# Three of eight experts computed in plain float32, with the raw weights as the stationary operand of the matmuls

## The chip, the core and the metric

The kernel runs on one core of a Trainium2 chip. The metric is the device time of one execution in microseconds (us). Before the change the median of three runs is 1679.45 us (1677.75 to 1680.64). Inside the core, TensorE (PE) multiplies matrices, and its weight loads are a row of their own in the profile (PEld); VectorE (DVE) and ScalarE (ACT) do elementwise work; GpSimd (POOL) does a little; SyncE (SP) issues the transfers (DMA) from HBM, the chip's main memory.

## The reference

The reference is a trunk of two layers over 256 tokens of width 1024, all in float32. Layer 0 has a mixer, a cross-attention to memory tokens and a dense SwiGLU; layer 1 has another mixer, another cross-attention, and a mixture of eight SwiGLU experts of width 3584. This last part, on the normalised tokens `t`, takes the second half of the time:

```
logits = t @ w_router                       # 256 x 8
top_v, top_i = top_k(logits, 2)             # two experts per token
combine = one_hot(top_i) * softmax(top_v)   # weight of each expert for each token
for e in range(8):
    out += combine[:, e] * ((silu(t @ wg[e]) * (t @ wu[e])) @ wd[e])
```

The weights of an expert are 1024x3584 (gate), 1024x3584 (up) and 3584x1024 (down). All eight have to be read, about 352 MB in float32.

## The kernel before, in words

**Number format.** [...] To hold the precision the kernel splits each operand into a high and a low part: `wh` is the rounded weight, which ACT writes (line 120, two calls of 1024 columns for a piece), and `wl` is the remainder, which DVE writes (line 122, one call of 2048 columns). A piece is 1 MB of weights, 128x2048, in one of 13 `raw` buffers; three pairs of `wh`/`wl` exist (pool `wsplit`, `bufs=3`). A product is then three matmuls: high by high (line 137), low activations by high weights (line 140), high activations by low weights (line 143), in `mm3`.

**Experts.** A token goes to two experts only. The kernel sorts the experts by how many tokens chose them (`places`, line 859) and puts them at positions 0 to 7 of the loop `for e in range(NE)`. Positions in `SMALL` take the three experts with the fewest tokens, with 64 slots for tokens (`SCAP`); the others have 128 slots (`CAP`). If an expert had more, code behind the loop would do the rest; it is not entered here.

**Chunks.** Each expert runs in seven chunks of 512 of its 3584 columns. A chunk reads six pieces: gate (two halves), up (two halves), down (two halves). `gate_up` multiplies the gathered tokens by gate and up; `gated` applies SiLU and the product; `to_hT` transposes the result; `down` multiplies the previous chunk's result by the down weights into `yacc`. So PE's order in a chunk is gate, up, the down of the chunk before, transposes.

**Large experts.** The tokens are the stationary operand (128 slots wide), and 512 columns of the weights move past them. A chunk is 24 matmuls for gate, 24 for up and 24 for down, each of 512 columns.

**Small experts, before.** The high and the low part of 64 slots lie side by side in one stationary tile of 128 columns, so that a product needs two matmuls (`mm2`, line 985: by `wh`, by `wl`): 16 for gate, 16 for up, 16 for down. ACT copies both results to SBUF (`sgs`, line 1019); eight float32 matmuls by the constant `twice` (line 1036) transpose them and add the two halves; then SiLU (line 1038), the product (line 1039) and a split (`hs`, lines 128 and 129).

**Around the experts.** `gather_pair` (line 934), in the last chunk of every second expert, picks the tokens of the next two experts by matmuls with one-hot matrices; `slot_rstd` (line 963) fetches the norm factor of each slot; `slots_T` (line 972) and `scatter` (line 1066) add an expert's result back to the residual `x`.

**Order.** The order of instructions on each engine is written when the program is built and is the same in each execution; an engine takes its instructions strictly in that order and waits when an operand is not there. SP issues the loads of the pieces in turn, and waits before each for the release of the `raw` buffer that it fills.

Of the kernel before, what the change touches and what calls it, by code (L numbers as in the profile page):

```python
# [11 lines left out]
F32 = mybir.dt.float32  # L12
# [22 lines left out]
SCAP = 64  # L35
SMALL = (2, 4, 6)
LAM_INIT = 0.8 - 0.6 * math.exp(-0.3)
# [17 lines left out]
def trunk_kernel(ctx: ExitStack, tc: tile.TileContext, io, out, stop=None):  # L55
# [151 lines left out]
    def route_consts():  # L207
# [20 lines left out]
        nc.gpsimd.iota(iota, pattern=[[1, P]], base=0, channel_multiplier=0, allow_small_or_imprecise_dtypes=True)  # L228
        iota2 = cp.tile([P, 2, SCAP], F32, tag="iota2", name="iota2")
        nc.gpsimd.iota(iota2, pattern=[[0, 2], [1, SCAP]], base=0, channel_multiplier=0,  # L230
                       allow_small_or_imprecise_dtypes=True)
        place = cp.tile([P, 4, 2], F32, tag="place", name="place")
        nc.gpsimd.iota(place, pattern=[[1, 4], [4, 2]], base=0, channel_multiplier=0,
                       allow_small_or_imprecise_dtypes=True)
        return wr, gc, tri, ustr, ones, iota, iota2.rearrange("p a b -> p (a b)"), place.rearrange("p a b -> p (a b)")

    pA = ctx.enter_context(tc.tile_pool(name="acts", bufs=1))
    ps2 = ctx.enter_context(tc.tile_pool(name="xs", bufs=2))
    with ExitStack() as pre:
# [526 lines left out]
        with behind("resid", "Pool"):  # L766
            wr, gc, tri, ustr, ones, iota, iota2, place = route_consts()
        mem_v_half(1, 0)
# [3 lines left out]
    with ExitStack() as moe:  # L772
# [140 lines left out]
        def slots(dst, t, e):  # L913

            at = byp[:, t, e:e + 1] if ids[1] is not None else pos[:, t, e:e + 1]
            chain["DVE"] = nc.vector.tensor_scalar(dst, iota2 if e in SMALL else iota, at, None, op0=OP.is_equal)

        def gained(kk, e, n, src):

            dh, dl = (xg_all[i][:, 0:n, kk, :] for i in range(2))  # L920
            g1 = gc[:, kk:kk + 1]
            chain["ACT"] = nc.scalar.activation(dh, src, AF.Copy, scale=g1)
            for i in range(n):
                if e + i in SMALL:
                    dst = hi = dh[:, i, SCAP:P]
                    rows = src[:, i, SCAP:P]
                else:
                    dst, hi, rows = dl[:, i, :], dh[:, i, :], src[:, i, :]
                chain["DVE"] = nc.vector.scalar_tensor_tensor(dst, rows, g1, hi.bitcast(F32), op0=OP.mult, op1=OP.subtract)

# [3 lines left out]
        def gather_pair(e):  # L934

            n = min(2, NE - e)
            se = m2.tile([P, 2, 2, P], F32R, tag="sg", name="sp", bufs=1)
            for t in range(2):
                for i in range(2):
                    slots(se[:, t, i, :], t, min(e + i, NE - 1))  # L940
            for q in range(4):
                if q < 2:
                    ps = mbank([P, 2, 2, P], "xg")
                else:
                    ps = accp.tile([P, 2, 2, P], F32, tag="acc", name="xg")
                for k in range(2):
                    kk = 2 * q + k
                    sl = slice(kk * P, (kk + 1) * P)
                    for t in range(2):
                        nc.tensor.matmul(ps[:, k, :, :], xh[t][:, sl], se[:, t, :, :], start=t == 0, stop=False)  # L950
                        nc.tensor.matmul(ps[:, k, :, :], xl[:, t, sl], se[:, t, :, :], start=False, stop=t == 1)
                    gained(kk, e, n, ps[:, k, 0:n, :])

# [3 lines left out]
        def one_hot(e):  # L957
            se = m2.tile([P, 2, P], F32, tag="sg", name="so", bufs=1)
            for t in range(2):
                slots(se[:, t, :], t, e)  # L960
            return se
# [10 lines left out]
        def slots_T(e):  # L972
            se = one_hot(e)
            tp = mbank([P, 2, P], "setp")
# [3 lines left out]
            nc.scalar.activation(st, tp, AF.Copy)  # L978
            return st

        def gate_piece(w, e, c, half):
            return load_w(w[ids[e], half * 512:(half + 1) * 512, c * 512:(c + 1) * 512]
                          .rearrange("(k p) n -> p k n", p=P), 4, 512)

        def mm2(jobs, first, last):

            for which in range(2):
                for i, (ps, a, *b) in enumerate(jobs):
                    f = first and which == 0 and all(j[0] is not ps for j in jobs[:i])
                    e = last and which == 1 and all(j[0] is not ps for j in jobs[i + 1:])  # L990
                    mm = nc.tensor.matmul(ps, a, b[which], start=f, stop=e)  # L991
            return mm

        def gate_up(e, c, xg, ready=(), between=None):
            xgh, xgl = xg
            res = []
            ready = list(ready)
            for w in (wg, wu):
# [4 lines left out]
                for half in range(2):  # L1003
                    wh, wl = ready.pop(0) if ready else gate_piece(w, e, c, half)
                    if e in SMALL:
                        mm = mm2([(ps, xgh[:, half * 4 + k, :], wh[:, k, :], wl[:, k, :]) for k in range(4)],
                                 half == 0, half == 1)
                    else:
                        mm = mm3([(ps, xgh[:, half * 4 + k, :], xgl[:, half * 4 + k, :], wh[:, k, :], wl[:, k, :])
                                  for k in range(4)], False, half == 0, half == 1)  # L1010
                res.append(ps)
# [14 lines left out]
        def down_w(e, c, parts=1):  # L1026
            return [load_w(wd[ids[e], c * 512 + half * 256:c * 512 + half * 256 + 256, :]
                           .rearrange("(k p) n -> p k n", p=P), 2, D, parts) for half in range(2)]

        def to_hT(e, sg, pool=pA, tag="gain"):  # L1030
            if e in SMALL:

                tp = mbank([P, 2, 4, SCAP], "htp")
                for i in range(2):
                    for k in range(4):
                        nc.tensor.matmul(tp[:, i, k, :], sg[:, i, k * P:(k + 1) * P], twice, start=True, stop=True)
                h = m2.tile([P, 4, SCAP], F32, tag="hsm", name="hsm", bufs=1)
                nc.scalar.activation(h, tp[:, 0, :, :], AF.Silu)
                nc.vector.tensor_tensor(h, h, tp[:, 1, :, :], op=OP.mult)
                hs = pool.tile([P, 4, P], F32R, tag=tag, name="hs")  # L1040
                chain["hh"], chain["hl"] = split_to(hs[:, :, 0:SCAP], hs[:, :, SCAP:P], h)
                return hs, None
            tp = mbank([P, 4, P], "htp")
# [7 lines left out]
        def down(c, hT, yacc, w2, ns=(0, 1)):  # L1051
            hh, hl = hT
            if hl is None:
                return mm2([(yacc[n], hh[:, half * 2 + k, :], w2[half][0][:, k, n * 512:(n + 1) * 512],
                             w2[half][1][:, k, n * 512:(n + 1) * 512])
                            for half in range(2) for n in ns for k in range(2)], c == 0, c == nch - 1)
            return mm3([(yacc[n], hh[:, half * 2 + k, :], hl[:, half * 2 + k, :],
# [3 lines left out]
        def split_y(yacc, n, pool=mA, tag="y"):  # L1061
            y = pool.tile([P, 2, 512], F32R, tag=tag, name="y")
            split_to(y[:, 0, :], y[:, 1, :], yacc[n])
            return y
# [47 lines left out]

        twice = mA.tile([P, SCAP], F32, tag="twice", name="twice")
        for i in range(2):
            nc.gpsimd.tensor_copy(twice[i * SCAP:(i + 1) * SCAP, :], ident[i * SCAP:(i + 1) * SCAP, i * SCAP:(i + 1) * SCAP])
        prev = y = st = nrs = pyacc = gf = None
        for e in range(NE):
            for c in range(nch):
# [3 lines left out]
                def between():  # L1122
# [4 lines left out]
                    elif c == 4:  # L1127
                        st = slots_T(e)
                    elif c == nch - 1 and e + 1 < NE:
                        nrs = slot_rstd(e + 1)  # L1130
# [28 lines left out]
                if c == 0:  # L1159
                    yacc = [mmp.tile([P, 512], F32, tag="mm", name=f"y{n}") for n in range(2)]  # L1160
                hT = to_hT(e, sg) if e + 1 < NE or c + 1 < nch else to_hT(e, sg, mA, "y")
# [130 lines left out]
```

## Time and profile before

| what | value |
|---|---|
| median of three runs | 1679.45 us |
| the profiled execution's own time | 1674.53 us |
| its span (first to last instruction) | 1672.8 us |
| PE busy, matmuls | 1581.7 us (95%) |
| PE busy, weight loads | 1300.4 us (78%) |
| DVE busy | 1263.6 us (76%) |
| ACT busy | 1077.1 us (64%) |
| TensorE clock granted, mean | 0.996 |
| read from HBM | 461.90 MB |

The span starts and ends with instructions; the execution's own time is 1.7 us longer. The profiled execution is 4.9 us below the median of the runs shown. The eight experts take about the last 1030 us. [...]

### The profile page before, as it was taken

The page shows a single profiled execution, that of the slowest core. Times are in us where ns is not written, and L with a number is a line of the kernel's source. Part 1 is how long each engine was busy: PE and PEld are TensorE (multiplying, and loading weights), DVE is VectorE, ACT ScalarE, POOL GpSimd, SP SyncE. Part 2 cuts the span into 40 slices and gives each one's busy share as a digit, 9 for nine tenths or more (in the row PEclk, how much of TensorE's full clock was granted, in tenths as well). Part 3 has the DMA queues.
Part 4 walks back from the last instruction along what each step waited for, and adds up shares of the span by engine and source line. Part 5 has one row for each costly group of instructions (what it writes and reads, how often), then busy time and mean ns, then how long its engine had stood idle before and what let it go on. Part 6 is the DMA issues. An engine that isn't in the chain of part 4 may idle for free. (4 is left out here: it accounts for less than half of the span.)

```text
span 1672.8 us, 22375 instructions
## 1 busy us (share of the span) xinstructions
PE 1581.7 (95%) x8448; PEld 1300.4 (78%) x8448; DVE 1263.6 (76%) x1214; ACT 1077.1 (64%) x1396; POOL 46.9 (3%) x68
## 2 busy tenths in 40 slices
PE   8999999999999999999999889998889998889996
PEld 7799889999988888888887567776557776557774
DVE  5785664454586658989888789788779878878876
ACT  5555553443564447877777777777777667778765
POOL 1010010000000102000000000000000000000000
PEclk9999999999999999999999999999999999999998
DMA  6556465555545597999999999999999999999960
GB/s 234 164 175 215 144 225 194 180 195 177 190 126 183 195 340 268 352 373 333 365 360 359 344 337 348 334 343 333 362 342 339 342 342 334 356 346 332 340 258 27
DMA packets 224560, 464.49 MB, mean 278 GB/s; under 512 B 9074, under 2 KB 64390, under 8 KB 224316
## 3 DMA queue, kind: packets, MB, share of 16 engines
q1 hardware_dynamic: 223564, 459.80, 78.1%
q0 software_dynamic: 880, 3.19, 0.6%
q8 instruction: 68, 1.11, 0.3%
q14 instruction: 48, 0.39, 0.1%
HBM read 461.90 MB, written 2.11 MB: 277 GB/s over the span
## 5 line engine op out<-in xcount | busy, mean ns | idle before, releaser
L122 DVE TENSOR_TENSOR wl<-raw,wh 128x2048 fp32r<-128x2048 f32 (+1 forms) x527 | 985.5, 1894 | 267.1 <-ACT wh L120 266.4
L120 ACT ACTIVATE wh<-raw 128x1024 fp32r<-128x1024 f32 x866 | 852.6, 1047 | 269.0 <-PE pws L140 94.9
L137 PE MATMUL gu<-wh,ch 128*128 128x512 f32 x560 | 222.0, 397 | 0.0
L140 PE MATMUL gu<-wh,cl 128*128 128x512 f32 x560 | 219.4, 392 | 0.1
L143 PE MATMUL gu<-wl,ch 128*128 128x512 f32 x560 | 155.8, 400 | 11.9 <-DVE wl L122 11.7
L143 PEld LDWEIGHTS gu<-wl,ch 128*128 128x128 f32 x560 | 101.7, 188 | 49.7 <-DVE wl L122 30.3
L140 PE MATMUL pws<-nl,wh 128*128 128x256 f32 x560 | 137.6, 283 | 0.0
L137 PE MATMUL pws<-nh,wh 128*128 128x256 f32 x560 | 137.6, 283 | 0.0
L991 PE MATMUL gu<-wl,ch 128*128 128x512 f32 x336 | 98.8, 416 | 40.1 <-DVE wl L122 40.1
L140 PEld LDWEIGHTS gu<-wh,cl 128*128 128x128 f32 x560 | 105.2, 188 | 22.2 <-DVE cl L1097 0.5
L137 PEld LDWEIGHTS gu<-wh,ch 128*128 128x128 f32 x560 | 105.2, 188 | 21.8 <-ACT hs L128 0.8
L137 PE MATMUL y<-wh,hs 128*128 128x512 f32 x280 | 112.9, 403 | 0.3 <-ACT wh L120 0.3
L991 PEld LDWEIGHTS gu<-wl,ch 128*128 128x128 f32 x336 | 57.3, 188 | 69.0 <-DVE wl L122 60.5
L140 PE MATMUL y<-wh,hs 128*128 128x512 f32 x280 | 110.4, 394 | 0.0
L137 PEld LDWEIGHTS pws<-nh,wh 128*128 128x128 f32 x560 | 106.2, 190 | 1.3 <-ACT wh L120 0.9
L140 PEld LDWEIGHTS pws<-nl,wh 128*128 128x128 f32 x560 | 106.1, 190 | 0.4
L991 PE MATMUL gu<-wh,ch 128*128 128x512 f32 x336 | 99.9, 403 | 1.5 <-ACT wh L120 1.3
L137 PE MATMUL acc<-wh,ch 128*128 128x512 f32 x216 | 84.7, 392 | 0.0
L140 PE MATMUL acc<-wh,cl 128*128 128x512 f32 x216 | 84.4, 391 | 0.0
L991 PEld LDWEIGHTS gu<-wh,ch 128*128 128x128 f32 x336 | 61.6, 188 | 22.7 <-ACT wh L120 10.2
L143 PE MATMUL pws<-nh,wl 128*128 128x256 f32 x560 | 78.8, 283 | 0.0
L143 PE MATMUL y<-wl,hs 128*128 128x512 f32 x280 | 74.6, 396 | 0.0
(363 smaller groups left out, 2197.4 us busy)
## 6 DMA issues: line engine op xcount, KB each, us to landing
raw<-in_moe_w_gate_dram SPq DMA_DIRECT2D x112, 1024.0 KB, 7.0
raw<-in_moe_w_up_dram SPq DMA_DIRECT2D x112, 1024.0 KB, 7.0
raw<-in_moe_w_down_dram SPq DMA_DIRECT2D x110, 1024.0 KB, 7.1
raw<-in_mem_w_kv_dram SPq DMA_DIRECT2D x16, 1024.0 KB, 5.5
raw<-in_odd_w_in_dram SPq DMA_DIRECT2D x12, 1024.0 KB, 5.2
raw<-in_ffn_w_gate_dram SPq DMA_DIRECT2D x11, 1024.0 KB, 5.2
raw<-in_ffn_w_up_dram SPq DMA_DIRECT2D x11, 1024.0 KB, 5.3
raw<-in_ffn_w_down_dram SPq DMA_DIRECT2D x11, 1024.0 KB, 4.7
```

The source lines that it names most:

```text
L120: chain["wh"] = nc.scalar.activation(hf[:, sl], rf[:, sl], AF.Copy)
L122: chain["wl"] = nc.vector.tensor_sub(lf[:, sl], rf[:, sl], hf[:, sl].bitcast(F32))
L137: mm = nc.tensor.matmul(ps, ah, bh, start=f, stop=False, skip_group_check=bank)
L140: nc.tensor.matmul(ps, *((ah, bl) if w_left else (al, bh)), start=False, stop=False, skip_group_check=bank)
L143: mm = nc.tensor.matmul(ps, *((al, bh) if w_left else (ah, bl)), start=False, stop=e, skip_group_check=bank)
L991: mm = nc.tensor.matmul(ps, a, b[which], start=f, stop=e)
```

## The change

The three small experts leave the split format. Their weights are no longer split: the `raw` piece itself is the stationary operand, in tiles of 128x128, and the 64 gathered tokens move past it, in plain float32. The gate, up and down results come out transposed (weights' columns on the partitions), so that the transposing matmuls, `sgs` and the split `hs` go. The norm factor of each slot is multiplied into the gathered tokens (`xsm`) rather than into the results. The accumulator `yacc` of a small expert is transposed back at its end (four transposes for each half, `split_y`). A chunk has 32 plain float32 matmuls for gate, 32 for up and 32 for down. The small positions move from 2, 4, 6 to 2, 4, 7, so that the order of experts is large, large, small, large, small, large, large, small. The last down weights are no longer loaded in two parts. The eight constants `place` are set one by one on POOL.

```diff
-SMALL = (2, 4, 6)
+SMALL = (2, 4, 7)
...
-        def gained(kk, e, n, src):
...
+        def gained(kk, e, n, src, rsrow):
+
             g1 = gc[:, kk:kk + 1]
-            chain["ACT"] = nc.scalar.activation(dh, src, AF.Copy, scale=g1)
             for i in range(n):
                 if e + i in SMALL:
...
+                    nc.vector.scalar_tensor_tensor(xsm[:, kk, :], src[:, i, 0:SCAP], g1, rsrow, op0=OP.mult, op1=OP.mult)
+                    continue
...
+            rsrow = None
+            for i in range(n):
+                if e + i in SMALL:
+                    sr = m2.tile([P, 2, SCAP], F32, tag="sr", name="sr", bufs=1)
+                    rp = mbank([P, SCAP], "rp")
+                    for t in range(2):
+                        nc.vector.tensor_scalar(sr[:, t, :], se[:, t, i, 0:SCAP].bitcast(F32), comb[:, t, NE:NE + 1], None, op0=OP.mult)
+                        nc.tensor.matmul(rp, ones, sr[:, t, :], start=t == 0, stop=t == 1)
...
+        def small_up(e, c, between):
+
+            ps = accp.tile([P, 2, 4, SCAP], F32, tag="acc", name="gu")
+            for i, w in enumerate((wg, wu)):
...
+                for half in range(2):
+                    r = load_raw(gate_src(w, e, c, half), 4, 512)
+                    for f in range(4):
+                        for k in range(4):
+                            chain["PE"] = nc.tensor.matmul(ps[:, i, f, :], r[:, k, f * P:(f + 1) * P], xsm[:, half * 4 + k, :],
+                                                           start=i == half == f == k == 0, stop=half == 1 and k == 3,
+                                                           skip_group_check=True)
+            return ps
...
             if e in SMALL:
-                sg = m2.tile([P, 2, 512], F32, tag="sgs", name="sgs", bufs=1)
-                for i in range(2):
-                    nc.scalar.activation(sg[:, i, :], res[i], AF.Copy, scale=rs)
-                return sg
+                h = m2.tile([P, 4, SCAP], F32, tag="hsm", name="hsm")
+                nc.scalar.activation(h, res[:, 0, :, :], AF.Silu)
+                nc.vector.tensor_tensor(h, h, res[:, 1, :, :], op=OP.mult)
+                return h
...
+                for half in range(2):
+                    for d in range(KT):
+                        for k in range(2):
+                            mm = nc.tensor.matmul(yacc[:, d, :], w2[half][:, k, d * P:(d + 1) * P], hh[:, half * 2 + k, :],
...
+                    yT[0] = m2.tile([P, KT, SCAP], F32, tag="yT", name="yT", bufs=1)
+                    nc.scalar.activation(yT[0], yacc, AF.Copy)
...
+                for k in range(4):
+                    nc.tensor.transpose(tp[:, k, :], yT[0][:, n * 4 + k, :], ident)
...
-        with behind("hh", "hl"):
-            w2 = down_w(pe, pc, 2)
+        w2 = down_w(pe, pc)
```

PE's order in the small expert at position 2, before: about one chunk in the middle of it. `gu` are the gate and up results, `y` the accumulator of down, `wh` and `wl` the split weights, `ch` the gathered tokens.

```order
L991 MATMUL gu<-wl,ch 128x512 x4
L991 MATMUL gu<-wh,ch 128x512 x3
L1036 MATMUL htp<-twice,sgs 128x64 x4
L991 MATMUL gu<-wl,ch 128x512 x4
L991 MATMUL gu<-wh,ch 128x512 x4
L991 MATMUL y_8179<-wh,hs 128x512
L991 MATMUL gu<-wl,ch 128x512 x4
L991 MATMUL y_8179<-wh,hs 128x512
L991 MATMUL y_8180<-wh,hs 128x512 x2
L1036 MATMUL htp<-twice,sgs 128x64 x4
```

The same place after the change; `raw` is the loaded piece, `xsm` and `hsm` the moving activations of 64 slots, `setp` belongs to `slots_T`.

```order
L1064 MATMUL y<-hsm,raw 128x64 x32
L1007 MATMUL gu<-xsm,raw 128x64 x64
L1064 MATMUL y<-hsm,raw 128x64 x32
L1007 MATMUL gu<-xsm,raw 128x64 x64
L1064 MATMUL y<-hsm,raw 128x64 x32
L1007 MATMUL gu<-xsm,raw 128x64 x32
L982 MATMUL setp<-ident,so 64x128 x2
L1007 MATMUL gu<-xsm,raw 128x64 x32
```

Fewer and wide matmuls, mixed with each other, have become 64 and 32 narrow ones in turn, with nothing of ACT's or DVE's splits in front of them.

ACT's order at the same position before: `wh` are the split weights, `hs` the split input of down.

```order
L120 ACTIVATE wh<-raw 128x1024 x4
L1019 ACTIVATE sgs<-gu,rs 128x512
L120 ACTIVATE wh<-raw 128x1024 x4
L1019 ACTIVATE sgs<-gu,rs 128x512
L120 ACTIVATE wh<-raw 128x1024 x2
L1038 ACTIVATE hsm<-htp 128x256
L120 ACTIVATE wh<-raw 128x1024 x2
L128 ACTIVATE hs<-hsm 128x4x64
```

And after, the whole small expert at position 2, up to the first splits for the large expert behind it; `ch` are the gathered tokens of that one.

```order
L1034 ACTIVATE hsm<-gu 128x256
L128 ACTIVATE y<-y_7277 128x512
L128 ACTIVATE y<-y_7278 128x512
L1034 ACTIVATE hsm<-gu 128x256 x3
L984 ACTIVATE st<-setp 64x256
L1034 ACTIVATE hsm<-gu 128x256 x2
L923 ACTIVATE ch<-xg,gc 128x128 x3
L1034 ACTIVATE hsm<-gu 128x256
L923 ACTIVATE ch<-xg,gc 128x128 x5
L120 ACTIVATE wh<-raw 128x1024 x6
```

ACT has one call of `hsm` for each of the seven chunks, and the splits of the next large expert (six calls, three pieces) stand behind all of them.

## Rows read from the trace of the kernel before

**Rows 1.** The page: busy time by engine, and the granted clock in 40 slices.
```profile
PE 1581.7 (95%) x8448; PEld 1300.4 (78%) x8448; DVE 1263.6 (76%) x1214; ACT 1077.1 (64%) x1396; POOL 46.9 (3%) x68
PEclk9999999999999999999999999999999999999998
```

**Rows 2.** Busy time by window: start:end, length, engines' busy, clock, DMA share, GB/s.
```profile
816.63:833.85 17.22, 17.22 (x80) 14.12 (x79) 15.27 (x11) 13.39 (x17) 0.00 (x0) 1.00 1.00 363
1046.24:1064.55 18.31, 17.36 (x76) 13.53 (x75) 14.74 (x9) 12.66 (x15) 0.00 (x0) 1.00 0.97 345
1174.26:1192.56 18.30, 15.04 (x65) 10.28 (x64) 14.41 (x9) 13.43 (x16) 0.00 (x0) 1.00 1.03 386
```

**Rows 3.** Who waited for whom, 645 to 1655 us: total, times, longest.
```profile
ACT sgs L1019 <- PE gu L991: 58.1, 36, 1.7
PE gu L991 <- DVE wl L122: 40.1, 56, 0.9
```

**Rows 4.** Timeline of ACT: start, length, line, operation, and idle before it.
```profile
867.74 0.67 ACT L1022 ACTIVATE sg<-gu,rs 128x512 f32<-128x512 f32 x1
...
1010.79 0.69 ACT L1022 ACTIVATE sg<-gu,rs 128x512 f32<-128x512 f32 x1 [0.48 <-PE gu L143]
1026.76 0.69 ACT L1022 ACTIVATE sg<-gu,rs 128x512 f32<-128x512 f32 x1 [1.72 <-PE gu L143]
...
1120.15 0.69 ACT L1022 ACTIVATE sg<-gu,rs 128x512 f32<-128x512 f32 x1 [2.07 <-PE rsp L967]
1138.46 0.69 ACT L1019 ACTIVATE sgs<-gu,rs 128x512 f32<-128x512 f32 x1 [1.72 <-PE gu L991]
...
1268.42 0.69 ACT L1022 ACTIVATE sg<-gu,rs 128x512 f32<-128x512 f32 x1 [0.45 <-PE gu L143]
...
1396.10 0.69 ACT L1019 ACTIVATE sgs<-gu,rs 128x512 f32<-128x512 f32 x1 [1.72 <-PE gu L991]
```

**Rows 5.** Timeline of PEld: runs of float32 weight loads, count at the end.
```profile
631.43 0.97 PEld L811 LDWEIGHTS rlp<-wr,rht 128*128 128x128 f32 x8
...
635.33 2.76 PEld L838 LDWEIGHTS xg<-se,h 128*128 128x128 f32 x24
...
890.38 1.09 PEld L1036 LDWEIGHTS htp<-twice,sgs 128*128 128x128 f32 x8
...
917.30 0.97 PEld L1036 LDWEIGHTS htp<-twice,sgs 128*128 128x128 f32 x8 [0.58 <-ACT sgs L1019]
```

**Rows 6.** Line 1036, both halves of a matmul: durations in ns (shortest/middle/longest).
```profile
L1036 PEld LDWEIGHTS htp<-twice,sgs x336: 186/192/192, 890.4 to 1518.4; 128*128 128x128 f32 x168
L1036 PE MATMUL htp<-twice,sgs x336: 217/275/323, 890.6 to 1518.4; 128*128 128x64 f32 x168
```

**Rows 7.** Timeline of PE: a large chunk's first down matmul, and the transposes behind its last.
```profile
820.87 0.40 PE L137 MATMUL y<-wh,hs 128*128 128x512 f32 x1
...
826.45 0.60 PE L1045 MATMUL htp<-ident,sg 128*128 128x128 f32 x4
```

**Rows 8.** Groups by line, whole span: the two gather matmuls of `gather_pair`.
```profile
L950 PE MATMUL xg<-sp,xh 128*128 128x256 f32 x64 | 15.6, 282 | 0.0
L951 PE MATMUL xg<-sp,xl 128*128 128x256 f32 x64 | 15.6, 281 | 0.0
```

**Rows 9.** The chain that ended last: the last matmuls of down.
```profile
1655.46 1.18 PE y L143 x5
```

**Rows 10.** Busy time by window: where the granted clock fell, and float32 loads.
```profile
550.00:552.00 2.00, 0.08 (x1) 0.12 (x1) 1.42 (x2) 0.00 (x0) 0.29 (x1) 1.00 0.58 179
553.00:554.00 1.00, 1.00 (x4) 0.81 (x3) 0.00 (x0) 0.00 (x0) 0.00 (x0) 0.50 0.80 248
...
631.00:633.00 2.00, 1.96 (x18) 1.96 (x19) 0.00 (x0) 1.57 (x5) 1.27 (x1) 1.00 0.00 0
```

**Rows 11.** Timeline of PE while the clock was at half.
```profile
554.20 0.63 PE L140 MATMUL pts<-wh,ml 128*128 128x512 f32 x1
554.63 0.63 PE L137 MATMUL pts<-wh,mh 128*128 128x512 f32 x1
```

More of the change, by code (lines that the diff above doesn't have):

```diff
@@ L228, in route_consts @@
         nc.gpsimd.iota(iota, pattern=[[1, P]], base=0, channel_multiplier=0, allow_small_or_imprecise_dtypes=True)
[L229 to L235, printed above, removed]
+        place = cp.tile([P, NE], F32, tag="place", name="place")
+        for i, r in enumerate((0, 4, 1, 5, 2, 6, 7, 3)):
+            nc.gpsimd.memset(place[:, i:i + 1], float(r))
+        return wr, gc, tri, ustr, ones, iota, place
     pA = ctx.enter_context(tc.tile_pool(name="acts", bufs=1))
@@ L951, in gather_pair @@
                         nc.tensor.matmul(ps[:, k, :, :], xl[:, t, sl], se[:, t, :, :], start=False, stop=t == 1)
[L952 removed]
+                    gained(kk, e, n, ps[:, k, 0:n, :], rsrow)
         wg, wu, wd = io["moe_w_gate"][0], io["moe_w_up"][0], io["moe_w_down"][0]
@@ L977, in slots_T, with gate_src, down_src @@
             st = m2.tile([P, 2, P], F32R, tag="st", name="st", bufs=1)
-            nc.scalar.activation(st, tp, AF.Copy)
-            return st
+            nc.scalar.activation(st[0:m], tp, AF.Copy)
+            return st[0:m]
+        def gate_src(w, e, c, half):
+            return w[ids[e], half * 512:(half + 1) * 512, c * 512:(c + 1) * 512].rearrange("(k p) n -> p k n", p=P)
         def gate_piece(w, e, c, half):
[L982 to L992, printed above, removed]
+            return load_w(gate_src(w, e, c, half), 4, 512)
+        def down_src(e, c, half):
+            return wd[ids[e], c * 512 + half * 256:c * 512 + half * 256 + 256, :].rearrange("(k p) n -> p k n", p=P)
+        def small_up(e, c, between):
+            ps = accp.tile([P, 2, 4, SCAP], F32, tag="acc", name="gu")
+            for i, w in enumerate((wg, wu)):
+                if i and between is not None:
+                    with behind("PE"):
+                        between()
+                for half in range(2):
[6 more added lines that the diff above has]
+            return ps
         def gate_up(e, c, xg, ready=(), between=None):
+            if e in SMALL:
+                return small_up(e, c, between)
             xgh, xgl = xg
@@ L1004, in gate_up @@
                     wh, wl = ready.pop(0) if ready else gate_piece(w, e, c, half)
[L1005 to L1010, printed above, removed]
+                    mm = mm3([(ps, xgh[:, half * 4 + k, :], xgl[:, half * 4 + k, :], wh[:, k, :], wl[:, k, :])
+                              for k in range(4)], False, half == 0, half == 1)
                 res.append(ps)
@@ L1026, in down_w @@
         def down_w(e, c, parts=1):
-            return [load_w(wd[ids[e], c * 512 + half * 256:c * 512 + half * 256 + 256, :]
-                           .rearrange("(k p) n -> p k n", p=P), 2, D, parts) for half in range(2)]
+            if e in SMALL:
+                return [load_raw(down_src(e, c, half), 2, D) for half in range(2)]
+            return [load_w(down_src(e, c, half), 2, D, parts) for half in range(2)]
         def to_hT(e, sg, pool=pA, tag="gain"):
             if e in SMALL:
[L1033 to L1042, printed above, removed]
+                return sg, None
             tp = mbank([P, 4, P], "htp")
@@ L1053, in down @@
             if hl is None:
-                return mm2([(yacc[n], hh[:, half * 2 + k, :], w2[half][0][:, k, n * 512:(n + 1) * 512],
-                             w2[half][1][:, k, n * 512:(n + 1) * 512])
-                            for half in range(2) for n in ns for k in range(2)], c == 0, c == nch - 1)
+                for half in range(2):
+                    for d in range(KT):
+                        for k in range(2):
+                            mm = nc.tensor.matmul(yacc[:, d, :], w2[half][:, k, d * P:(d + 1) * P], hh[:, half * 2 + k, :],
+                                                  start=c == half == d == k == 0, stop=c == nch - 1 and half == k == 1,
+                                                  skip_group_check=True)
+                return mm
             return mm3([(yacc[n], hh[:, half * 2 + k, :], hl[:, half * 2 + k, :],
@@ L1111, in final_gain @@
             return gf
-        twice = mA.tile([P, SCAP], F32, tag="twice", name="twice")
-        for i in range(2):
-            nc.gpsimd.tensor_copy(twice[i * SCAP:(i + 1) * SCAP, :], ident[i * SCAP:(i + 1) * SCAP, i * SCAP:(i + 1) * SCAP])
+        xsm = mA.tile([P, KT, SCAP], F32, tag="xsm", name="xsm")
+        yT = [None]
         prev = y = st = nrs = pyacc = gf = None
@@ L1128, in between @@
                         st = slots_T(e)
-                    elif c == nch - 1 and e + 1 < NE:
+                    elif c == nch - 1 and e + 1 < NE and e + 1 not in SMALL:
                         nrs = slot_rstd(e + 1)
@@ L1159, in trunk_kernel @@
                 if c == 0:
-                    yacc = [mmp.tile([P, 512], F32, tag="mm", name=f"y{n}") for n in range(2)]
+                    if e in SMALL:
+                        yacc = mmp.tile([P, KT, SCAP], F32, tag="mm", name="y")
+                    else:
+                        yacc = [mmp.tile([P, 512], F32, tag="mm", name=f"y{n}") for n in range(2)]
                 hT = to_hT(e, sg) if e + 1 < NE or c + 1 < nch else to_hT(e, sg, mA, "y")
```

26 lines of the change are left out of this document (16 added, 10 removed).

## The prediction

> **What bounds the kernel now.** I read the page first, then the windows, the waits, and the timelines of single engines. The page shows PE as the fullest engine at a clock that is full nearly everywhere [rows 1]. But a busy share is an average over three kinds of chunk, so the windows come next [rows 2]. A large chunk at position 1 takes 17.22 us and PE is busy in all of it: TensorE is the limit there. A small chunk takes 18.30 us with PE busy 15.04, its weight loads 10.28, DVE 14.41, ACT 13.43: no engine is full. A later large chunk takes 18.31 us and is not full either. The waits say why the small chunk is no shorter [rows 3]: ACT's `sgs` waits for PE (58.1 us, 36 times, 1.7 at the longest) and PE's matmuls by `wl` wait for DVE (40.1 us). ACT takes its instructions in order, so the splits behind `sgs` stand still too, and the loop ACT, DVE, PE, ACT sets the pace. Transfers are close behind: 345 to 386 GB/s in the windows of [rows 2], and 6.29 MB (six pieces of 1,048,576 bytes) at 386 GB/s are 16.3 us.
>
> So the splits are what a small chunk waits for. The question is what PE's own work becomes when they are gone.
>
> **What a plain float32 matmul costs.** The kernel already runs this very form: line 1036, stationary 128x128 and 64 moving columns, in float32. Its 168 matmuls (8 in each of 21 chunks) leave 336 records of each half, a load 0.19 us long [rows 6]: a float32 matmul is loaded and streamed twice. The step between two loads comes from the runs [rows 5]. The 24 of line 838, with 128 moving columns, take 2.76 us; less one load of 0.19 that is (2.76 - 0.19) / 23 = 0.1117 us. The 8 of line 1036 give (0.97 - 0.19) / 7 = 0.1114 with 64 columns, the 8 of line 811 the same 0.1114 with 8 columns. The step doesn't depend on the moving columns: the loads set it. One run of line 1036 is slower, (1.09 - 0.19) / 7 = 0.1286. I take 0.1117, from the longest run, and keep 0.1286 for the upper end.
>
> A small chunk then has 96 matmuls, 192 loads: 192 x 0.1117 = 21.45 us of PE, against 18.30 for all that a small chunk takes now. Before, it had 48 matmuls of 512 columns; 24 such matmuls take 826.45 - 820.87 = 5.58 us [rows 7], so 48 take 11.2, and the eight of line 1036 some 1.8. The change takes work from ACT and DVE, which were part of the loop, and puts about 8 us more on PE. PE is then the bound of the small experts, alone: gate, up and down of one small chunk are 7.15 us each, and SiLU and product (0.7 us and less on the idle ACT and DVE) lie beside the 7.15 us of the down matmuls.
>
> [...] The equal steps at 8, 64 and 128 columns in [rows 5] speak against counting columns here. [...]
>
> **The sum, stretch by stretch.** 21 small chunks are 4032 loads, 450 us. I follow PE between the gates' ends, which the SiLU or `sgs` calls of ACT mark [rows 4]. Below, 5.6 is a large expert's gate, up or down, 0.5 four transposes (0.60 less overlap, [rows 7]), 1.9 the eight matmuls of a scatter at 0.2325, 1.1 some ten small float32 records, 4 a gather. The gather's rows sum to 31.2 us over four gathers, 7.8 each [rows 8]; rows of neighbours overlap, so I take half.
>
> First small expert, from 867.74 to 1010.79, now 143.05 us. PE has to do: up 5.6, down 5.6, transposes 0.5, seven small chunks without the last down 150.2 - 7.15 = 143.0, the large expert's last down 5.6, scatter 1.9, small things 1.1, gather 4, the next gate 5.6. Sum 172.9, so +29.9. The next chunk, 1010.79 to 1026.76, is 15.97 now and becomes 5.6 + 7.15 + 0.5 + 0.5 + 5.6 = 19.35: +3.4.
>
> Rest of that large expert: unchanged. The order that I compared has PE's, ACT's and DVE's instructions of its later chunks exactly as before, ACT again with no piece split ahead, which is what separates 18.31 from 17.22 us in [rows 2]. Its last chunk into the small gate, 1120.15 to 1138.46, 18.31 us, becomes 5.6 + 5.6 + 0.5 + 7.15 = 18.85: +0.5.
>
> Second small expert, 1138.46 to 1268.42, 129.96 us: 150.2 less its first gate and last down, 135.9, then 5.6 + 1.9 + 1.1 + 4 + 5.6, together 154.1: +24.1, and +3.4 again in the chunk behind it.
>
> The rest, from 1396.10 to the end, 276.7 us, holds a small and a large expert whose places are exchanged. The large one first: as position 5 now, 1396.10 - 1268.42 = 127.7, and 4 for the gather that now falls into it. Then the small one: 143.0 + 5.6 + 1.9 + 0.3, and 1.2 for the broadcast of the final gain. The end: from the last down matmul, 1655.46 + 1.18 = 1656.6 [rows 9], to 1672.8 are 16.2, plus a copy of 512 columns, 0.7 as `sgs` in [rows 4], and 0.5 for transposes. Sum 301.1: +24.4. Placing a small expert last gains nothing: its last down is longer (7.15 for 5.6) and must be transposed.
>
> Total 29.9 + 3.4 + 0.5 + 24.1 + 3.4 + 24.4 = 85.7 us. Against the profiled execution's own time, 1674.5, that is 1760.2; the median of the runs shown is 4.9 above that execution, so I expect **1765 us**.
>
> The rest at nothing. POOL's eight `memset` calls are on an engine that is busy for 3% of the span [rows 1], ahead of the routing. The extra matmuls and copies for `rsrow` in the first `gather_pair` stand in a large chunk, one or two us at the most if PE waits for them. `xsm` has one buffer: DVE can't write the next small expert's tokens until the last gate and up of this one are through, and ACT's and DVE's gather work is queued behind it; it lies beside a 7.15 us down, and costs 2 us in each of two places if that cover is too short. SP's loads now wait for PE to release `raw` instead of DVE: six pieces in 21.45 us are 293 GB/s, under every rate in [rows 2], so transfers get slack.
>
> **Rivals.**
>
> *Loads hidden (faster).* If in long unbroken runs the next load slides fully under the running matmul, PE takes 192 x 64 columns at 0.2325 / 512, or 5.6 us, and the small chunk falls to the transfers, 16.3 to 17.3 us at 386 to 363 GB/s [rows 2]. Then 21 x (18.3 - 16.8) = 31 us are won: 1648. It decides from a step under 0.095 us (18.3 / 192). Against it stand the runs of 24 and 8, which are unbroken too. Chance 0.06.
>
> *The clock falls.* [...] Chance 0.08.
>
> *Slower steps.* 0.1286 for all loads [rows 5] is 4032 x 0.0169 = 68 us more, 1833; half of it, 1799. Chance 0.10.
>
> *Quick large chunks.* PE arrives from a small expert late, with ACT's splits waiting, as at position 1. If that lasts, 21 large chunks take 17.22 instead of 18.31: -23, 1742. Against it: the same order of instructions. Chance 0.14.
>
> **How the numbers follow.** The forecast holds 0.60, with 1750 to 1780 as its own range; the remaining 0.02 is for no change. The range takes in quick large chunks with some margin and the half-way case of slower steps: 1728 to 1815. The clock, the hidden loads and the worst steps, about 0.2, stay outside. A change of under 0.2%, 3.4 us, can't be told from none. Faster: 0.06. Same: 0.02. Slower: 0.92.
>
> **What would show it.** In the profile after: loads `gu<-xsm,raw` and `y<-hsm,raw` with a step near 0.112 us; PEld full in the small experts; about 150 us for seven small chunks; DVE and ACT nearly idle there; GB/s under 300; large chunks behind them still at 18.3 us; a granted clock of 1.00. A step of 0.06, or a clock of 0.5, would make the prediction wrong.

## The result and the profile after

The changed kernel takes 1814.74 us (median of four runs, 1803.97 to 1817.39); the kernel before, on the same chip, takes 1678.97 (1677.75 to 1680.64). The ratio is 1.080, 95% interval 1.075 to 1.084: 136 us slower. The forecast was 1765 with a range of 1728 to 1815: the result lies 0.3 us under its upper end, and two of the four executions lie above it. The profiled execution took 1817.39 us, its span 1815.7.

First the page after, against [rows 1]:

```profile
PE 1768.7 (97%) x11160; PEld 1575.9 (87%) x11160; DVE 979.7 (54%) x1065; ACT 802.3 (44%) x1080; POOL 46.1 (3%) x72
PEclk9899999999999999999999899999999999999965
GB/s 241 126 193 189 161 216 192 188 179 196 140 186 170 329 279 359 343 363 365 313 280 293 232 317 334 343 278 292 291 264 315 339 351 329 346 279 280 253 72 25
```

DVE and ACT have each lost some 280 us of work, as the change meant. PE and PEld have gained 187 and 276. And the row of the clock, all nines but its last slice in [rows 1], has an 8 in slice 2, another in slice 23, and ends in 6 and 5. The GB/s fall below 300 wherever a small expert runs.

The windows give the size of a chunk, in the columns of [rows 2]: a small chunk, a later large chunk, then the last chunk of the last (small) expert.

```profile
986.38:1007.82 21.44, 21.44 (x194) 21.44 (x194) 0.42 (x1) 0.38 (x1) 0.00 (x0) 1.00 0.88 297
1094.82:1113.14 18.32, 17.91 (x78) 13.82 (x77) 15.43 (x9) 12.66 (x15) 0.00 (x0) 1.00 0.88 318
1749.00:1760.00 11.00, 11.00 (x53) 11.00 (x54) 0.00 (x0) 0.00 (x0) 0.00 (x0) 0.50 0.00 0
1760.00:1780.00 20.00, 20.00 (x96) 20.00 (x95) 0.42 (x1) 0.38 (x1) 0.00 (x0) 0.50 0.00 1
```

The small chunk is 21.44 us, PE and PEld full, DVE and ACT nearly idle, clock 1.00: the forecast's 21.45 to within a hundredth. The last two rows show the same work, PE as full, at clock 0.50, with nothing to wait for. PE's timeline around them (start, duration, what):

```profile
1716.99 14.46 PE L1007 MATMUL gu<-xsm,raw 128*128 128x64 f32 x128
1731.29 7.31 PE L1064 MATMUL y<-hsm,raw 128*128 128x64 f32 x64
1738.53 1.98 PE L1130 MATMUL gfp<-gfrow,ones 1*128 1x512 f32 x4
1740.43 27.12 PE L1007 MATMUL gu<-xsm,raw 128*128 128x64 f32 x128
1767.35 27.52 PE L1064 MATMUL y<-hsm,raw 128*128 128x64 f32 x128
```

The same 128 records of gate and up take 14.46 us before `gfp` and 27.12 behind it; `gfp` are the matmuls that spread the final gain from one partition to 128. The two downs behind them take 27.52. The clock never came back before the end.

A smaller fall of the same kind stands at the gather in the first small expert:

```profile
1018.00:1021.00 3.00, 3.00 (x29) 3.00 (x29) 0.00 (x0) 0.00 (x0) 0.00 (x0) 1.00 0.85 275
1021.00:1024.00 3.00, 2.27 (x21) 2.21 (x21) 1.27 (x7) 0.00 (x0) 0.00 (x0) 1.00 0.85 279
1024.00:1027.00 3.00, 3.00 (x18) 3.00 (x16) 0.00 (x0) 0.00 (x0) 0.00 (x0) 0.53 0.83 313
1027.00:1033.00 6.00, 6.00 (x30) 6.00 (x30) 0.46 (x2) 0.37 (x1) 0.00 (x0) 0.50 0.20 52
1033.00:1036.00 3.00, 3.00 (x23) 3.00 (x22) 1.10 (x5) 0.63 (x2) 0.00 (x0) 0.77 0.67 259
```

Behind four matmuls of one moving column PE pauses 0.73 us (3.00 - 2.27) for the one-hot tiles of the gather, which DVE writes; then the clock is at half for 10 us, and comes back behind nine gather matmuls of 256 columns (1031.1 to 1033.2). The second small expert has the same for 6.8 us, from 1321.1. In the last expert, between its last matmuls of 512 columns and `gfp`, the same thin matmuls (but for two transposes) held 1.00 for 96.7 us:

```profile
1641.84:1738.53 96.69, 96.69 (x868) 96.62 (x866) 3.25 (x7) 2.30 (x6) 0.00 (x0) 1.00 0.77 261
```

### The profile page after: what moved, and what is told of

It reads as the page before. It is cut to its first block, busy times and chain, and to the rows that moved or that the text cites. A ratio compares the mean times of both kernels' runs of the same rounds, so it can differ in the third digit from the quotient of the medians.

```text
span 1815.7 us, 27052 instructions
## 1 busy us (share of the span) xinstructions
PE 1768.7 (97%) x11160; PEld 1575.9 (87%) x11160; DVE 979.7 (54%) x1065; ACT 802.3 (44%) x1080; POOL 46.1 (3%) x72
## 5 line engine op out<-in xcount | busy, mean ns | idle before, releaser
L122 DVE TENSOR_TENSOR wl<-raw,wh 128x2048 fp32r<-128x2048 f32 (+1 forms) x399 | 700.9, 1780 | 216.8 <-ACT wh L120 215.7
L120 ACT ACTIVATE wh<-raw 128x1024 fp32r<-128x1024 f32 x610 | 603.5, 1051 | 269.2 <-PE pws L140 99.1
L1007 PEld LDWEIGHTS gu<-xsm,raw 128*128 128x128 f32 x2688 | 322.3, 201 | 1.8 <-ACT gf L1131 0.8
L1007 PE MATMUL gu<-xsm,raw 128*128 128x64 f32 x2688 | 323.4, 284 | 0.0
L137 PE MATMUL gu<-wh,ch 128*128 128x512 f32 x560 | 222.2, 397 | 1.4 <-ACT wh L120 1.4
L143 PE MATMUL gu<-wl,ch 128*128 128x512 f32 x560 | 156.0, 400 | 12.2 <-DVE wl L122 11.8
L1064 PE MATMUL y<-hsm,raw 128*128 128x64 f32 x1344 | 166.4, 289 | 0.0
L1064 PEld LDWEIGHTS y<-hsm,raw 128*128 128x128 f32 x1344 | 165.4, 205 | 0.4
L143 PEld LDWEIGHTS gu<-wl,ch 128*128 128x128 f32 x560 | 101.5, 188 | 47.1 <-DVE wl L122 28.2
L137 PEld LDWEIGHTS gu<-wh,ch 128*128 128x128 f32 x560 | 105.1, 188 | 24.7 <-ACT wh L120 2.3
```

Source lines behind the costliest of these rows:

```text
L120: chain["wh"] = nc.scalar.activation(hf[:, sl], rf[:, sl], AF.Copy)
L122: chain["wl"] = nc.vector.tensor_sub(lf[:, sl], rf[:, sl], hf[:, sl].bitcast(F32))
L137: mm = nc.tensor.matmul(ps, ah, bh, start=f, stop=False, skip_group_check=bank)
L143: mm = nc.tensor.matmul(ps, *((al, bh) if w_left else (ah, bl)), start=False, stop=e, skip_group_check=bank)
L1007: chain["PE"] = nc.tensor.matmul(ps[:, i, f, :], r[:, k, f * P:(f + 1) * P], xsm[:, half * 4 + k, :], start=i == half == f == k == 0, stop ...
L1064: mm = nc.tensor.matmul(yacc[:, d, :], w2[half][:, k, d * P:(d + 1) * P], hh[:, half * 2 + k, :], start=c == half == d == k == 0, stop=c = ...
```

## The experiments

Two theories. **Clock:** the float32 step is as forecast, and what came on top is TensorE's clock: thin float32 (64 moving columns) holds a full clock but doesn't bring back a lost one, so that a small disturbance can cost many microseconds. **Not the clock:** the excess is in the placement, the gathers or the transfers, and the clock only shows it.

**1. Take the disturbance away.** The final gain is spread by a DMA, without `gfp`:

```diff
-                nc.tensor.matmul(ps, ones[0:1, :], row[:, n * 512:(n + 1) * 512], start=True, stop=True)
+            nc.sync.dma_start(gf, bcast(io["norm_final"], 0, [[1, D]]))
```

> The final gain is spread over the partitions by a DMA and no longer by PE's four one-row matmuls (gfp, 1738.53 to 1740.43 in the profile after, right ahead of the fall of the clock at 1741). Theory A: these few rows, in the middle of float32 matmuls of 64 columns, cost the full clock, and 64-column float32 holds a full clock but doesn't bring it back. Then the last 256 float32 records run at 0.112 instead of 0.21 us: 54.6 us become 28.6, and the end some 3 us shorter: 1786 us. Rival B: a long run of 64-column float32 loses the clock by itself after a while: the fall stays, 1810 to 1817.

Measured: 1792.24 us, ratio 1.064 (1.058 to 1.070). In its trace the last gate and up take 14.46 us again, and so do the last downs:

```profile
1752.25 14.46 PE L1007 MATMUL gu<-xsm,raw 128*128 128x64 f32 x128
1766.55 14.46 PE L1064 MATMUL y<-hsm,raw 128*128 128x64 f32 x128
```

That is 22.5 us less, and the falls at the gathers are still there (20.5 and 17.1 us long in this execution).

**2. Undo the placement.** `SMALL` and `place` as before, a large expert last:

```diff
-SMALL = (2, 4, 7)
+SMALL = (2, 4, 6)
```

> The changed kernel with the small experts back at positions 2, 4, 6, so that a large one is last. Theory A: the one-row matmuls fall among matmuls of 512 columns and cost no clock; three small experts cost about 88 us as forecast, and each of them some 3 to 5 us of half clock at its gather: 1775 to 1785. Rival B (the clock is lost by long runs alone): a fall in or behind position 6 that lasts until its end, 1795 or more. If the place of the small expert itself cost the time (its longer end, nothing hidden behind it), the clock would be as before and the time still under 1790: then the profile's clock tells.

Measured: 1800.39 us, ratio 1.071 (1.068 to 1.075): too high by 15 to 25. `gfp` now stands among matmuls of 512 columns and the clock stays up there. But it was at half for 17.1 us at each of two gathers:

```profile
1311.00:1314.00 3.00, 2.27 (x21) 2.21 (x21) 1.27 (x7) 0.00 (x0) 0.00 (x0) 1.00 0.88 286
1314.00:1331.00 17.00, 17.00 (x85) 17.00 (x85) 2.54 (x9) 1.75 (x5) 0.00 (x0) 0.52 0.38 119
1331.00:1335.00 4.00, 4.00 (x34) 4.00 (x34) 1.81 (x8) 0.99 (x3) 0.00 (x0) 0.90 0.68 249
```

So the loss isn't tied to `gfp`. But a pause alone doesn't decide it either: at the first of the three gathers of this execution PE pauses for the same 0.73 us, and the clock stays at 1.00.

```profile
1020.00:1023.00 3.00, 2.27 (x21) 2.21 (x20) 1.27 (x7) 0.00 (x0) 0.00 (x0) 1.00 0.89 272
1023.00:1026.00 3.00, 3.00 (x29) 3.00 (x28) 0.00 (x0) 0.00 (x0) 0.00 (x0) 1.00 0.74 283
```

Whether the clock falls at a gather, and how long it stays down, differs between executions; what decides it stays open. This gives a comparison at equal order of PE's instructions: the stretch of the first small expert (start of `sg` to start of `sg`) took 172.30 us here without a fall, 177.06 in the changed kernel with 10.2 us at half clock, and 181.85 in experiment 1 with 20.5 us. The starts here, then in experiment 1:

```profile
874.05 0.67 ACT L1038 ACTIVATE sg<-gu,rs 128x512 f32<-128x512 f32 x1
1046.35 0.69 ACT L1038 ACTIVATE sg<-gu,rs 128x512 f32<-128x512 f32 x1 [3.69 <-PE gu L143]
876.76 0.67 ACT L1038 ACTIVATE sg<-gu,rs 128x512 f32<-128x512 f32 x1
1058.61 0.69 ACT L1038 ACTIVATE sg<-gu,rs 128x512 f32<-128x512 f32 x1 [3.70 <-PE gu L143]
```

Undoing the placement is worth 14 us; the rest of the loss stays.

**3. Halve PE's work.** Every second contraction of the small experts is left out (half of their sums); all weights are still loaded.

```diff
-                        for k in range(4):
+                        for k in (0, 3):
```

> Leaves out half of each small expert's contractions (two of four k in gate and up, one of two in down), so half of its matmuls; all weights are still loaded from HBM. PE has 96 loads a small chunk, 10.7 us at full clock. If the clock stays full, the chunk falls to the transfers, about 17 us, and the time to 1700 to 1720 us. Theory A says that 64-column float32 doesn't bring a clock back once it is lost, and with PE waiting for transfers it will be lost: then 96 x 0.209 = 20.1 us a chunk, 1780 to 1795 us with the granted clock at 0.5 in the small experts.

Measured, one run: 1598.17 us, below both. I had taken some 16 us of transfers for the floor of a small chunk. Its windows of two small chunks:

```profile
905.02:915.74 10.72, 10.72 (x98) 10.72 (x98) 0.42 (x1) 0.38 (x1) 0.00 (x0) 1.00 1.04 397
915.74:926.46 10.72, 10.72 (x98) 10.72 (x98) 0.42 (x1) 0.38 (x1) 0.00 (x0) 1.00 1.04 387
```

10.72 us are 96 x 0.1117: PE's loads set these chunks alone. At 390 GB/s a chunk of 10.72 us brings in 4.2 of its 6.29 MB; I take the rest to be pieces loaded ahead in the `raw` buffers while large chunks ran. PE waited for a transfer seven times, 4.2 us in all. The half clock of Theory A came only in places: for 20.5 us from 955.8, for 17.1 us from 1184.4, and from 1549.7, behind `gfp`, to the end.

**4. Twice the columns.** Gate and up move their 64 slots twice, 128 columns, and their results take two accumulators in place of one:

```diff
-   nc.tensor.matmul(ps[:, i, f, :], r[:, k, f * P:(f + 1) * P], xsm[:, half * 4 + k, :],
+   nc.tensor.matmul(ps[i][:, f, :, :], r[:, k, f * P:(f + 1) * P], xsm[:, half * 4 + k, None, :].to_broadcast([P, 2, SCAP]),
```

> Gate and up of the small experts move 128 columns instead of 64 (the 64 slots twice, the second copy is not used); the loads are the same. If the loads set the step, a small chunk stays at 21.4 to 21.6 us; if columns count, gate and up get longer by up to 6.8 us a chunk, 28 us. The clock: if it is the thin columns that make it fall, it stays at 1.00 in gate and up and at the gather, and the time falls to about 1775 to 1790 us; if it is the one-row matmuls alone, the last expert's fall stays, 1805 to 1817.

Measured, one run: 1775.42 us, with a small chunk of 21.44 again. The clock doesn't fall at the gathers; behind `gfp` it falls and is back at once:

```profile
939.24:960.68 21.44, 21.44 (x194) 21.44 (x193) 0.42 (x1) 0.38 (x1) 0.00 (x0) 1.00 0.88 295
1722.00:1725.00 3.00, 3.00 (x16) 1.95 (x15) 0.00 (x0) 1.19 (x2) 0.00 (x0) 0.93 0.00 0
1725.00:1728.00 3.00, 3.00 (x16) 3.00 (x16) 0.00 (x0) 0.00 (x0) 0.00 (x0) 0.51 0.03 5
1728.00:1740.00 12.00, 12.00 (x110) 12.00 (x109) 0.28 (x1) 0.38 (x1) 0.00 (x0) 1.00 0.00 0
```

Doubling the columns leaves the step as it was, and this run is 39 us below the changed kernel. Not all of that is the clock: with the second accumulator PE's order changed too. At the gather the changed kernel (first line) paused; here (second and third) 64 matmuls of gate or up stand right behind the four of one column, and there is no pause.

```profile
1023.20 0.36 PE L955 MATMUL xg<-sp,xh 128*128 128x256 f32 x1 [0.73 <-DVE sp L913]
1025.02 0.50 PE L972 MATMUL rsp<-comb,so 128*128 128x1 f32 x4
1025.39 7.39 PE L1007 MATMUL gu<-xsm,raw 128*128 128x128 f32 x64
```

So that the clock stays up at the gathers doesn't show here what the columns do; that it is back at once behind `gfp`, where the order is the same, does.

**5. Both edits (1 and 4) at once.**

> The changed kernel with both edits at once: gate and up of the small experts move their 64 slots twice (128 columns), and the final gain is spread by a DMA in place of the float32 matmuls gfp. Theory A (the loss beyond 1765 us is TensorE's half clock, which thin float32 work lets in at the gathers and at gfp): 1768 to 1778 us, no stretch at half clock after 700 us longer than 4 us. Theory B (the loss comes from the transfers or the gathers and the single run at 1775 was luck): 1790 to 1805 us, as with the final gain by a DMA alone.

Measured: 1768.08 us, ratio 1.052 (1.049 to 1.055). Its row of the clock:

```profile
PEclk9899999999999999999999999999999999999998
```

No slice among the experts is under 9. The change without its loss of clock is within 3 us of the forecast of 1765, in part by luck. Between the profiled executions of the changed kernel and of this one, 47.2 us apart, about 11 us aren't clock but the other order: 6.6 us less in the large experts behind small ones, and two pauses each of 0.73 and 1.42 us that are gone.

**6. One chunk only.** To rule out that the other 20 wide chunks helped, only the last one, behind `gfp`, is wide:

```diff
+            wide = e == NE - 1 and c == nch - 1
```

> The changed kernel, where in one chunk of 21, the last (it starts behind the final gain's matmuls gfp), gate and up move the 64 slots twice, 128 columns; gfp stays where it is. Theory A (after gfp the clock falls either way, but a float32 matmul of 64 columns doesn't bring it back and one of 128 does): the clock falls at gfp and is back within 10 us, the last chunk takes 21.4 to 25 us in place of 36, the fall in the end goes and the time is 1782 to 1800. Theory B (the wider matmuls of the other 20 chunks, before gfp, were what kept the end quick in the fully wide kernel): the clock stays at 0.50 to the end, 1808 to 1818.

Measured: 1785.36 us, ratio 1.065 (1.060 to 1.070). The windows behind `gfp`:

```profile
1732.00:1736.00 4.00, 4.00 (x20) 2.69 (x19) 0.00 (x0) 1.19 (x2) 0.00 (x0) 0.90 0.00 0
1736.00:1738.00 2.00, 2.00 (x12) 2.00 (x11) 0.00 (x0) 0.00 (x0) 0.00 (x0) 0.50 0.00 0
1738.00:1750.00 12.00, 12.00 (x107) 12.00 (x107) 0.00 (x0) 0.38 (x1) 0.00 (x0) 0.98 0.00 1
1750.00:1764.00 14.00, 14.00 (x128) 14.00 (x127) 0.42 (x1) 0.00 (x0) 0.00 (x0) 1.00 0.00 1
```

The clock falls behind `gfp` as in the changed kernel, comes back within 4 us under float32 matmuls of 128 columns, and the thin down matmuls behind them (from 1750) hold it. Up to `gfp` PE's order from the first small expert on is that of the changed kernel, record by record; behind it the last gate, up and downs take 30.4 us (1734.30 to 1764.73) in place of 54.4, so the columns of one chunk are worth 24 us. For the last expert "Not the clock" is out; for the gathers the three lengths of one stretch in experiment 2 say the same.

**7. Less of the change, to beat both.** Gate and up stay split; only down goes to plain float32:

```diff
+            if e in SMALL:
+                return [load_raw(src[half], 2, D) for half in range(2)]
```

> The kernel before with one part of the change alone: the small experts' gate and up stay split (512 columns moving), only their down product is in plain float32 with the raw weights stationary; the small experts stand in their old places. Theory A (PE's work sets a small chunk, and each float32 weight load costs 0.1117 us): 32 split matmuls at 5.58 / 24 = 0.2325 us are 7.44 us, 16 loads of the two transposes 1.8 us, 64 loads of down 7.15 us, together 16.4 us against 18.30 before; 24 small chunks at 1.9 us give back 45 us, so 1625 to 1655 us. Theory B (what holds a small chunk at 18.30 us is not PE but the transfers or the split work on DVE and ACT): transfers ran at up to 395 GB/s with half the PE work, so a chunk can't fall under some 16 us, and if the order of the splits holds it the time stays at 1670 to 1685. If the half clock comes in with the 64-column float32 of down, up to 30 us come back on top, and the profile shows clock 0.50 at the gathers.

Measured: 1776.10 us, ratio 1.057 (1.055 to 1.059), far off both. (There are 21 small chunks, not the 24 that the sum counts.) The waits (total, times, longest) and one window:

```profile
DVE hs L1044 <- ACT hsm L1042: 108.0, 19, 8.2
ACT hsm L1042 <- PE htp L1040: 84.8, 19, 5.1
```

```profile
965.00:970.00 5.00, 3.89 (x12) 3.05 (x12) 5.00 (x3) 2.61 (x3) 0.00 (x0) 0.59 0.66 217
```

The transposes `htp` stood on PE behind 7 us of down where there had been 3.7; ACT's `hsm` waited, the next splits behind it too, PE then paused, and the clock fell: 0.59 in this window, 0.966 over the span against 0.996 before.

**8 and 9. Mend the order.** First the second half of down goes behind `to_hT`:

```diff
+                        down(pc, phT, nacc, w2, halves=(0,))
+                        hT = to_hT(e, sg)
+                        down(pc, phT, nacc, w2, halves=(1,))
```

> As the run before with only down in plain float32, but in a small expert the transposing matmuls of a chunk (htp) now stand between the two halves of the down product, not behind all 7 us of it. That run took 1776 where 1640 was hoped for: ACT's hsm waited 5.1 us for htp with the next chunk's splits queued behind it, PE then waited for those splits, and the clock fell to half for 6.8 us in each chunk. Theory A (the order alone, with the half clock that its pauses let in, cost the 135 us): hsm waits under 2.5 us, hardly any half clock in the small experts, a small chunk 16.4 to 18.3 us, 1635 to 1685 us. Theory B (the mix of thin float32 and split matmuls is slow whatever the order): small chunks stay above 20 us, 1740 to 1780 us.

Measured: 1744.30 us, ratio 1.039 (1.037 to 1.042). Now DVE waited for the one buffer of `hs`:

```profile
DVE hs L1044 <- PE y L1060: 122.0, 16, 8.6
```

So `hs` gets two places in its tile:

```diff
+                hs = hs2[0][:, c % 2, :, :]
```

> The run before (1744 us), with two places for the product hs in place of one. There DVE waited 8.6 us in each small chunk for the last down matmul to release hs, with the splits wl queued behind it, and ACT's sgs then waited 5.2 us for PE. Theory A (that wait is what is left of the loss): hs waits under 1 us, a small chunk 16.4 to 18.3 us in place of 20.4, the half clock of 3.4 us in each chunk gone, 1640 to 1690 us. Theory B (thin float32 of the down product in between keeps the clock falling): chunks stay above 19.5 us, 1720 to 1745 us.

Measured: 1707.82 us, ratio 1.016 (1.013 to 1.019). A small chunk inside an expert, and the chunk behind the expert:

```profile
964.53:981.82 17.29, 17.15 (x116) 14.88 (x115) 9.81 (x8) 9.61 (x12) 0.00 (x0) 1.00 0.98 361
1022.05:1044.39 22.34, 19.81 (x121) 16.64 (x120) 10.62 (x7) 9.84 (x13) 0.00 (x0) 1.00 0.86 300
```

The steady chunk beats the 18.30 of [rows 2] by 1 us, but the chunk behind is 6.4 us longer than its 15.97 before, and the first chunks of each small expert run late too. I had counted only the steady chunk.

**10 and 11. Fewer changes between the kinds.** The small experts go to places 5, 6 and 7, once all in split format, once with the edits of 7 to 9:

```diff
+        for i, r in enumerate((0, 4, 5, 6, 7, 1, 2, 3)):
+            nc.gpsimd.memset(place[:, i:i + 1], float(r))
```

> The kernel before, all in split format, with the three small experts moved to the last three places (5, 6, 7) and the five large ones ahead of them; nothing else. Theory A (a large chunk takes 17.22 us as long as none but large ones have run, and 18.31 only behind a small expert, because ACT's and DVE's splits fall behind there): the 21 large chunks of the places 2 to 4 take 17.2, 21 x 1.1 = 23 us are won, 1650 to 1660 us. Theory B (a large chunk takes 18.3 later on for another reason, such as the transfers): 1670 to 1685 us, no change.

> The run with down in plain float32 and two places for hs (1707.8 us), with the three small experts in places 5, 6, 7. Theory A: its small chunks run at 17.29 us against 18.30, but each way into and out of a small expert costs some 10 us; with one way in and none out, and large chunks at 17.22 ahead, 1630 to 1655 us, faster than before. Theory B (large chunks take 18.3 anyway and the gathers keep the losses): 1675 to 1700 us.

Measured: 1686.03 us, ratio 1.004 (1.0025 to 1.0057), and 1707.77 us, ratio 1.018 (1.016 to 1.020). In the first, large chunks at positions 1, 2 and 3, before any small expert has run:

```profile
837.11:854.06 16.95, 16.95 (x78) 13.91 (x77) 14.69 (x8) 13.12 (x15) 0.00 (x0) 1.00 1.00 350
940.40:959.23 18.83, 18.35 (x81) 14.02 (x80) 15.09 (x11) 12.93 (x16) 0.00 (x0) 1.00 0.93 329
1053.38:1071.69 18.31, 17.68 (x77) 13.65 (x76) 15.19 (x9) 12.66 (x14) 0.00 (x0) 1.00 0.95 332
```

Large chunks sink from 17 to some 18.3 us by themselves; small experts aren't the cause, and what is these runs don't say. In the second kernel the chunks around each change from one small expert to the next still took 21.5 to 23.3 us. No version beat the kernel before.

## Why the prediction was right, and where it was off

**Inside the range by luck.** The direction and the larger part of the time came out as worked out, but that 1814.74 lies under 1815 is luck: the upper end was set for half-way slower steps (1799), which didn't come, and what filled the space, half clock, was put outside the range with a chance of 0.08. The forecast's own range, 1750 to 1780, was missed by 35 us.

**The step: right.** 192 loads at 0.1117 were to give 21.45 us; 21.44 was measured, at 64 columns and, in experiment 4, at 128. The loads set it, as [rows 5] said.

**What it removes: right.** DVE and ACT at 0.42 and 0.38 us in a small chunk, large chunks further behind unchanged at 18.3, transfers at 297 GB/s.

**The sum, by its stretches.** Span to span the change adds 142.9 us in the profiled pair, against 85.7 forecast. The stretches run between the starts of ACT's calls, as in [rows 4]; after, the second gate's end is `hsm` less one 7.15 us product. The starts after:

```profile
875.47 0.67 ACT L1038 ACTIVATE sg<-gu,rs 128x512 f32<-128x512 f32 x1
1052.53 0.69 ACT L1038 ACTIVATE sg<-gu,rs 128x512 f32<-128x512 f32 x1 [3.68 <-PE gu L143]
1074.71 0.69 ACT L1038 ACTIVATE sg<-gu,rs 128x512 f32<-128x512 f32 x1 [2.55 <-PE gu L143]
1194.56 0.38 ACT L1034 ACTIVATE hsm<-gu 128x256 f32<-128x256 f32 x1 [13.42 <-PE gu L1007]
1346.50 0.69 ACT L1038 ACTIVATE sg<-gu,rs 128x512 f32<-128x512 f32 x1 [5.84 <-PE gu L143]
1481.00 0.69 ACT L1038 ACTIVATE sg<-gu,rs 128x512 f32<-128x512 f32 x1 [1.71 <-PE gu L143]
```

| stretch | forecast | measured | the difference |
|---|---|---|---|
| start to the first small expert (867.74 became 875.47) | 0 | +7.7 | half clock, below |
| first small expert (177.1 for 143.05) | +29.9 | +34.0 | half clock at the gather, 10.2 us |
| chunk behind it (22.18 for 15.97) | +3.4 | +6.2 | PE waits, see the small miss |
| rest of that large expert, into the small gate | +0.5 | +1.0 | |
| second small expert (159.1 for 129.96) | +24.1 | +29.1 | half clock at the gather, 6.8 us, and some 1.6 us unexplained |
| large expert behind it (134.5 for 127.7) | +3.4 | +6.8 | PE waits, the same |
| the rest (334.7 for 276.7) | +24.4 | +58.0 | half clock from `gfp` to the end |

**What failed: the clock.** The forecast said a granted clock of 1.00, and priced its fall at nothing. The last stretch is off by 33.6 us: (27.12 - 14.46) + (27.52 - 14.46) = 25.7 of it are the last gate, up and downs, by the rows of experiment 1, and the tail behind them, at 0.50, is 20.8 us, 3.4 longer than forecast; it was 19.8 and 19.5 in experiments 1 and 6, where the clock fell only some 5 us into it, so a little over 1 us of the 3.4 is the clock's. The other 4.5 are the large expert before it (2.3), PE's wait of 1.42 us for `wh` in the first small chunk, and `gfp`, 1.98 us for 1.2. The gathers are 4.1 and 5.0 over; without a fall the first small expert takes 172.30 us (experiment 2), and 172.9 were forecast. The rival *The clock falls*, at 0.08, named the cause. The two microseconds of float32 loads at 1.00 in [rows 10] were no test of whether such work brings a fallen clock back. Float32 of 64 columns held the clock here (1.00 for 96.7 us in one stretch) and didn't restore it (54 us at 0.50 with PE full). Each of these falls came behind a small disturbance, a pause of 0.73 us or four float32 matmuls on one partition; but such a pause didn't always bring one (the first gather in experiment 2, 0.73 us, and 1.42 us at 1622 in the changed kernel). Nor does busy time, as the profile shows it, explain it: behind `gfp` PE was busy for 54.43 of 54.47 us, and the clock stayed at 0.50.

**A small miss.** The chunk behind a small expert was summed as PE's work alone, 19.35; PE was busy 19.65 of 22.18. The six splits that ACT had ahead are three pieces of six; PE waited 2.5 us in each of two places, 1.8 of it for the splits of the others and 0.7 for ACT's copy `yT` ahead of the transposes.

**The start.** From 44.5 on the profiled execution shows 17.1 us at half clock, long before anything that the change touches, and the first expert arrives 7.7 us later. The rows of the clock of experiments 1, 2, 4, 5 and 9 have an 8 in the same slice, those of 3 and 7 and of the kernel before a 9. So it goes with the execution; what decides it stays open.

**The other rivals.** Hidden loads and slower steps are out by the 21.44. Quick large chunks are out by the 18.3, which experiment 10 showed to arise without small experts. The forecast's end, "placing a small expert last gains nothing", held, and cost more than said.

## What to carry to other kernels

Count plain float32 matmuls by their weight loads, not by their columns: the 192 loads of a small chunk took 21.44 us with 64 moving columns, and again with 128 in gate and up. Narrow moving operands paid the full load each time, so unsplit float32 is dear exactly where few tokens make the split format look wasteful. Where PE runs on thin float32, look in the row of the granted clock behind each gather, broadcast or pause: padding the moving operand to 128 columns cost no time in the step here, and in the one chunk behind `gfp` it gave back 24 us. And before ordering a longer product ahead of a transpose, ask which engine's queue waits behind that transpose.

## What the hardware showed that I had not expected

- PE and PEld fully busy with float32 matmuls of 64 columns left the clock at 0.50 for 54 us, while the same work held 1.00 for 96.7 us; 128 columns brought it back within 4 us (experiment 6). What decides it these runs don't say.
- The same pause of 0.73 us at the same place of PE's order cost the clock in one execution and not in another: the stretch around it took 172.30, 177.06 and 181.85 us with 0, 10.2 and 20.5 us at half clock.
- Doubling the moving columns of a float32 matmul from 64 to 128 changed the step by nothing: 21.44 us for the chunk both times.
- With half of PE's work, one core read 397 and 387 GB/s in two chunks, above the 386 that [rows 2] show at the most.
